# Second values and gates moved into the attention loop's background, later queries placed by transfers, background weights split in one piece

## Chip, cores and metric

The kernel runs on one core of one Trainium2 chip, as one program and one launch. The metric is the device time in microseconds (us), lower is better: the median of several executions. The profile is of one more execution of the same program, with a time of its own.

## What is computed

A decoder trunk of two layers on 512 tokens of width 1024, in float32. Layer A is a gated short convolution and an MLP. Then one shared key/value side is projected (`w_kv`, six parts of 256 columns: raw, selection and window keys and values). Layer B is an attention with 16 heads in 4 groups over three branches, followed by another MLP and a last norm. Cut to what bears on the change:

```python
kv = (h @ w_kv).reshape(B, S, 6, N_KV_GROUPS, HEAD_DIM)
k_cmp = compress_blocks(k_raw, cmp_pe_k, phi_k_w1, phi_k_w2)   # blocks of 32 tokens, stride 16
v_cmp = compress_blocks(v_raw, cmp_pe_v, phi_v_w1, phi_v_w2)   # silu(flat @ w1) @ w2
qg = h @ w_qg                                                  # 1024 query + 48 gate columns
q = qg[..., :1024] * HEAD_DIM ** -0.5
gates = sigmoid(qg[..., 1024:])
# for every query: softmax over compressed blocks, over selected blocks, over the window
o = gt[..., 0:1] * o_c + gt[..., 1:2] * o_s + gt[..., 2:3] * o_w
return o.reshape(B, S, 1024) @ w_o
```

With 512 tokens all selection blocks are taken, so the selection and the window branch are both full causal attentions (`br` 0 and 1) with keys and values of their own.

## The kernel before, in words

Every float32 matmul is made of three float16 matmuls on a high and a low half of each operand. So each weight piece is loaded by a DMA on SP's queue (`load_piece`, L188 to L201, three buffers `wst`), and `convert_piece` (L210) makes its high half on ScalarE (L232, `whi`) and its low half on VectorE (L233, `wlo`, four buffers of each). The list `pieces` (L122 to L140) is the order in which pieces are loaded, converted and used. A piece has 1024 columns per partition, two of them carry 256 output columns of a projection. Pieces with an index below `whole` (L139) are converted in two steps of 512, those from there on in one step of 1024 (`ahead_fine`, L839). Conversion runs two pieces ahead of use.

The attention section starts at L760. A **lead-in** (L1080) runs to its end piece by piece: `keys(0)`, `keys(1)` (selection and window keys into `KD`), `queries(0)` (group 0), `values(0)`, `values(1)` (L865, into `VT`: 96 matmuls of 256 columns, in two accumulation banks, then four evictions of 128x256 on ScalarE and on VectorE, L883 and L884), `gates()` (L887: 96 matmuls of 48 columns, then four sigmoids, L899).

Then the **loop of items** (L1318) starts. An item is one pass of scores for one group, one block of 128 queries, one branch and one, two or four heads (`Full`, L1132, 22 for each group), or one pass over compressed blocks for two groups (`Cmp`, L1207, 8 of them), 96 items in all. Its stages: `st0` makes scores on TensorE into bank `b`, adds the bias on VectorE (L1160) and takes the exponential on ScalarE (L1162); `st1`, two items later, transposes the weights on TensorE into bank `c` (L1168, two banks) and copies the high half on ScalarE (L1171); `st2`, three items later, makes the low half on VectorE (L1174), which frees the bank; `st3`, four items later, multiplies with the values (L1187 to L1189) and, at the end of a block, weights by the gates; `st4`, six items later, turns a finished block for the output projection.

Beside the items runs a **background** (L1303), a chain of generators that is given TensorE work by a credit: in each pass of the loop `credit` rises (L1334) and generators are stepped until it is used up, where a step is worth about its TensorE time in us. The chain: `raw(0)`, `queries(1)`, `phi(0)` alternating with `raw(1)`, `queries(2)`, `phi(1)`, `queries(3)`, and when groups 0 and 1 are finished (mark `o1`) `out_proj(0)`. `raw` (L933) projects raw keys or values, scales them in another order (L946), splits them (L409) and puts them with 12 DMAs (L952 to L954) into the tile `big`, from which `phi` (L960, 96 matmuls of 155 columns) reads. `queries(g)` (L906) makes the query tile `Q` (three buffers): the head's own half by a copy on ScalarE (L917) and the other half by a subtraction (L918) on VectorE for groups 1 and 2, on GpSimd for 0 and 3; these heads stand in a list `later`, and one is taken out in each pass.

The order on each engine is not exactly that of the program: it is set when the program is built, by dependences and readiness. `first_half` and `mlp_down` of the second MLP follow the attention.

## Time and profile before

| | us |
|---|---|
| median of 3 runs | 1106.68 (1106.1 to 1107.04) |
| the profiled execution, its own time | 1106.44 |
| its span | 1104.7 |
| TensorE matmul busy in the span | 1087.0 (98%) |
| VectorE busy | 897.3 (81%) |
| ScalarE busy | 584.0 (53%) |
| GpSimd busy | 57.4 (5%) |
| granted TensorE clock, mean | 0.998 |

How to read it: times are from the span's start. Matmuls are pipelined and their ends are modelled, so a busy TensorE (PE) is not one without gaps: a gap shorter than a matmul's tail does not show as idle. DVE is VectorE, ACT is ScalarE, POOL is GpSimd, SP is the engine whose queue issues most transfers, PEld is the load of a matmul's weights. In a row of `--lines` kind, the numbers after the bar are busy us and mean ns of one instruction, then the engine's idle time before them and what ended it. The lead-in's last part lies between about 521 and 544.8 us, the loop of items between 544.8 and 752 us, the output projection and the second MLP behind that.

### The profile page before, as it was taken

Reading aid. Unit: us, or ns where it says so; the run is one execution under the profiler, and the core shown is the slowest. Engines: PE = TensorE matmul, PEld = TensorE weight load, DVE = VectorE, ACT = ScalarE, POOL = GpSimd, SP = SyncE. Lnnn points to the kernel's source line nnn. Section 1 sums busy time; section 2 is a strip of 40 time slices with the busy share of each in tenths; the row PEclk is TensorE's granted clock in tenths of the full one; section 3 lists DMA queues with packets and bytes.
Section 4 is the critical chain, followed back from the end, with each engine's and each line's share of the span. In section 5 each row is a group of like instructions: output and inputs, shape, how many; then the busy total and the mean of one; then the engine's idle time right before and its main releaser. Section 6 shows DMA issues by size and latency. Waiting matters only on the chain. (4 is left out here: it accounts for less than half of the span.)

```text
span 1104.7 us, 20302 instructions
## 1 busy us (share of the span) xinstructions
PE 1087.0 (98%) x8112; PEld 704.9 (64%) x8112; DVE 897.3 (81%) x1594; ACT 584.0 (53%) x925; POOL 57.4 (5%) x74
## 2 busy tenths in 40 slices
PE   9999999999999999999999999999999999999997
PEld 4446644447884448875767676675444788445886
DVE  5897757987988767979488899996798798875786
ACT  5663245544333544447677887874655534352353
POOL 1000000000000000000100102211100000000022
PEclk9999999999999999999999999999999999999999
DMA  8353135633333333312352432011653333330222
GB/s 254 117 152 115 39 96 153 172 96 115 115 108 106 111 97 108 103 31 76 115 154 68 131 116 79 28 33 57 172 153 115 116 115 115 115 96 1 84 89 77
DMA packets 149710, 115.77 MB, mean 105 GB/s; under 512 B 8828, under 2 KB 146768, under 8 KB 149616
## 3 DMA queue, kind: packets, MB, share of 16 engines
q1 hardware_dynamic: 146720, 109.14, 33.0%
q10 hardware_dynamic: 2512, 4.70, 1.4%
q8 instruction: 64, 1.05, 0.4%
q0 software_dynamic: 384, 0.63, 0.2%
q14 instruction: 30, 0.25, 0.1%
HBM read 110.22 MB, written 2.14 MB: 102 GB/s over the span
## 5 line engine op out<-in xcount | busy, mean ns | idle before, releaser
L232 ACT ACTIVATE whi<-wst 128x1024 f16<-128x1024 f32 (+3 forms) x156 | 136.2, 887 | 120.8 <-PE b L387 37.4
L688 PEld LDWEIGHTS <-whi 128*128 128x128 f16 x1768 | 173.0, 98 | 20.4
L219 ACT ACTIVATE whi<-wst 128x1792 f16<-128x1792 f32 x70 | 118.2, 1696 | 124.6 <-DVE wst L160 55.5
L233 DVE SCALAR_TENSOR_TENSOR wlo<-wst,whi 128x1024 f16<-128x1024 f32 (+3 forms) x156 | 157.1, 1017 | 26.6 <-ACT whi L232 26.3
L388 PEld LDWEIGHTS <-wlo 128*128 128x128 f16 x976 | 95.5, 98 | 105.5 <-issue 0.7
L386 PEld LDWEIGHTS <-whi 128*128 128x128 f16 x976 | 95.7, 98 | 101.0 <-issue 0.9
L387 PEld LDWEIGHTS <-whi 128*128 128x128 f16 x976 | 95.5, 98 | 100.3 <-issue 0.3
L220 DVE SCALAR_TENSOR_TENSOR wlo<-wst,whi 128x1792 f16<-128x1792 f32 x70 | 141.0, 2018 | 15.4 <-ACT whi L219 15.4
L625 DVE TENSOR_TENSOR rl<-ml_z,rh 128x1792 f16<-128x1792 f32 x32 | 64.7, 2023 | 44.5 <-ACT rh L624 44.4
L688 PEld LDWEIGHTS <-wlo 128*128 128x128 f16 x884 | 86.5, 98 | 10.8 <-issue 0.4
L624 ACT ACTIVATE rh<-ml_z 128x1792 f16<-128x1792 f32 x32 | 54.3, 1696 | 60.2 <-DVE ml_z L166 60.2
L1162 ACT ACTIVATE at_p<-at_s,at_m 128x384 f32<-128x384 f32 (+3 forms) x128 | 70.9, 555 | 22.3 <-DVE at_m L1160 21.2
L388 PE MATMUL b<-xsh,wlo 128*128 128x512 f16 x208 | 78.8, 379 | 0.0
L387 PE MATMUL b<-xsl,whi 128*128 128x512 f16 x208 | 78.8, 379 | 0.0
L386 PE MATMUL b<-xsh,whi 128*128 128x512 f16 x208 | 78.8, 379 | 0.0
L386 PE MATMUL c<-xsh,whi 128*128 128x512 f16 x192 | 72.8, 379 | 0.0
L387 PE MATMUL c<-xsl,whi 128*128 128x512 f16 x192 | 72.8, 379 | 0.0
L388 PE MATMUL c<-xsh,wlo 128*128 128x512 f16 x192 | 72.8, 379 | 0.0
L158 DVE TENSOR_TENSOR wst<-wst 128x512 f32<-128x512 f32 x70 | 48.5, 695 | 26.5 <-DMA wst<-mlp_w_dram 25.2
L688 PE MATMUL a<-rh,whi 128*128 128x256 f16 x256 | 69.1, 273 | 0.0
L688 PE MATMUL a<-rh,wlo 128*128 128x256 f16 x256 | 69.1, 273 | 0.0
L688 PE MATMUL c<-rh,whi 128*128 128x256 f16 x252 | 68.7, 273 | 0.1
(388 smaller groups left out, 2686.8 us busy)
## 6 DMA issues: line engine op xcount, KB each, us to landing
wst<-mlp_w_dram SPq DMA_DIRECT2D x256, 256.0 KB, 3.4
wst<-a_w_in_dram SPq DMA_DIRECT2D x12, 512.0 KB, 3.8
wst<-w_kv_dram SPq DMA_DIRECT2D x12, 512.0 KB, 3.8
wst<-a_w_out_dram SPq DMA_DIRECT2D x8, 512.0 KB, 3.4
wst<-b_w_qg_dram SPq DMA_DIRECT2D x8, 512.0 KB, 3.7
wst<-b_w_o_dram SPq DMA_DIRECT2D x8, 512.0 KB, 3.4
T<-ext_d ACTq DMA_DIRECT2D x6, 528.0 KB, 3.9
wst<-a_w_in_dram SPq DMA_DIRECT2D x12, 256.0 KB, 3.0
```

Source lines behind the costliest of these rows:

```text
L158: DVE.tensor_tensor(b[:, :, 4:7:2], b[:, :, 0:1].to_broadcast(two), b[:, :, 2:0:-1], op=OP.add)
L219: ACT.activation(hi, b[:, :, 1:], AF.Copy, scale=sc)
L220: lows[0] = DVE.scalar_tensor_tensor(lo, b[:, :, 1:], sc, hi, op0=OP.mult, op1=OP.subtract)
L232: ACT.activation(hi[:, s:e], w, AF.Copy, scale=sc)
L233: DVE.scalar_tensor_tensor(lo[:, s:e], w, sc, hi[:, s:e], op0=OP.mult, op1=OP.subtract)
L386: PE.matmul(ps, w[0], xs[0], start=start, stop=False, **k)
L387: PE.matmul(ps, w[0], xs[1], start=False, stop=False, **k)
L388: return PE.matmul(ps, w[1], xs[0], start=False, stop=stop, **k)
L624: ACT.activation(rh[0][:, p], z[:, 1:8], AF.Copy)
L625: DVE.tensor_tensor(rh[1][:, p], z[:, 1:8], rh[0][:, p], op=OP.subtract)
L688: mm = PE.matmul(acc7[i], wl if n == 1 else wh, xl if n == 2 else xh, stop=c == closes[i] and n == 2, start=c == 0 and n == 0 and not othe ...
L1162: self.weighed = ACT.activation(self.p[:, w], lg[:, w], AF.Exp, bias=mn[:, j:j + 1], scale=-1.0, accum_out=l[:, br * 4 + h:br * 4 + h + 1])
```

## The change

Two projections leave the lead-in and become the background's first: `values(1)` and `gates()`. A new check `need_last` lets a window item wait for them, in program order, before its `st3`. The background's order becomes `values(1)`, `gates()`, `queries(1)`, `raw(0)`, `phi(0)` alternating with `queries(2)`, `raw(1)`, `phi(1)`, `queries(3)`, `out_proj(0)`; the piece list is put into the same order. The credit per pass becomes 1.25 (items 0 to 53), 1.0 (to 63) and 0.75 instead of 1.14 (0 to 43), 0.9 (to 49) and 0.58. The first four `Cmp` items move from behind places 4, 7, 10, 13 of group 2 to behind 9, 11, 14, 16 (items 54, 57, 61, 64). For groups 1 to 3 a query tile's halves are made for two heads at a time on all 128 partitions (two copies, two subtractions) into `kr_hl`, and four DMAs on SP's queue put them in place. `raw` loses a memset and one of three DMAs of each group. `whole` moves from `queries(3)`'s pieces to those of `values(1)`, so all the background's pieces are converted in one step.

```diff
@@ -122,21 +122,21 @@
     block(b_w_qg[0], 0)
-    for part in (3, 5):
-        block(w_kv, part * 256)
+    block(w_kv, 3 * 256)
+    whole = len(pieces)
+    block(w_kv, 5 * 256)
     cols(b_w_qg[0], 1024, 48, SW)
+    block(b_w_qg[0], 256)
     block(w_kv, 0)
-    block(b_w_qg[0], 256)
     for k in (0, 8):
         block(phi_k_w1, 0, SW, k, 4)
-        cols(w_kv, 256, 256, SW, k // 2, 4)
+        cols(b_w_qg[0], 512, 256, SW, k // 2, 4)
         block(phi_k_w1, 0, SW, k + 4, 4)
     cols(phi_k_w2, 0, 64, SW, 0, 2)
-    block(b_w_qg[0], 512)
+    block(w_kv, 256)
     block(phi_v_w1, 0, SW, 0, 16)
     cols(phi_v_w2, 0, 64, SW, 0, 2)
-    whole = len(pieces)
     block(b_w_qg[0], 768)
@@ -886,15 +886,18 @@
         def gates():
             w = next_piece()
+            cv = ahead_fine()
             pg = abank()
             for t in range(4):
                 for c in range(8):
+                    next(cv, None)
...
-                yield
+                yield 0.6
+            drain(cv)
@@ -915,16 +918,30 @@
-                (POOL if g in (0, 3) else DVE).tensor_tensor(q[o, h], t[r, m], q[r, h], op=OP.subtract)
+                POOL.tensor_tensor(q[o, h], t[r, m], q[r, h], op=OP.subtract)
                 done.add(f"q{g}.{h}")
+            def two_heads(m, hl):
+                ACT.activation(hl[:, 2 * m], t[:, m], AF.Copy)
+                (POOL if g == 3 else DVE).tensor_tensor(hl[:, 2 * m + 1], t[:, m], hl[:, 2 * m], op=OP.subtract)
+            def put_heads(hl):
+                for s in range(2):
+                    r, o = slice(64 * s, 64 * s + 64), slice(64 - 64 * s, 128 - 64 * s)
+                    nc.sync.dma_start(q[r, s::2], hl[r, 0::2])
+                    nc.sync.dma_start(q[o, s::2], hl[r, 1::2])
+                done.update(f"q{g}.{h}" for h in range(4))
...
-            for h in range(4):
-                if lead_in[0]:
+            if lead_in[0]:
+                for h in range(4):
                     head(h)
-                else:
-                    later.append(lambda h=h: head(h))
+            else:
+                hl = ap.tile([128, 4, S], F16, name="kr_hl", bufs=1)
+                for m in range(2):
+                    later.append(lambda m=m: two_heads(m, hl))
+                later.append(lambda: put_heads(hl))
@@ -934,7 +951,6 @@
-            DVE.memset(kr[64:128, :, 0:4, S - 1:S], 0.0)
@@ -951,7 +967,6 @@
                     nc.sync.dma_start(kr[64:128, :, g, 0:S - 32], hl[r, :, 32:S])
-                    nc.sync.dma_start(kr[64:128, :, g, S - 32:S - 1], hl[r, :, 1:32])
@@ -1024,7 +1039,7 @@
-        done = set()
+        done = {"v0"}
@@ -1077,7 +1092,7 @@
-        for k in (keys(0), keys(1), queries(0), values(0), values(1), gates()):
+        for k in (keys(0), keys(1), queries(0), values(0)):
             drain(k)
@@ -1139,6 +1154,9 @@
+            def need_last(self):
+                return [f"v{self.br}"] + (["gates"] if self.br else [])
@@ -1295,16 +1316,18 @@
-        items += mixed(full(2), {4 + 3 * qb: Cmp(0, qb) for qb in range(4)})
+        items += mixed(full(2), {i: Cmp(0, qb) for qb, i in enumerate((9, 11, 14, 16))})
...
         def background():
+            yield from marked("v1", values(1))
+            yield from marked("gates", gates())
+            yield from queries(1)
             yield from raw(0)
-            yield from queries(1)
-            yield from in_turn(phi(0), raw(1))
-            yield from queries(2)
+            yield from in_turn(phi(0), queries(2))
+            yield from raw(1)
             yield from marked("cmp", phi(1))
...
-            credit += 1.14 if i < 44 else 0.9 if i < 50 else 0.58
+            credit += 1.25 if i < 54 else 1.0 if i < 64 else 0.75
...
+                        if s == 3:
+                            have(items[j].need_last())
                         getattr(items[j], f"st{s}")()
```

## Rows read from the trace of the kernel before

**Rows 1.** The page: busy us of each engine over the span.
```profile
PE 1087.0 (98%) x8112; PEld 704.9 (64%) x8112; DVE 897.3 (81%) x1594; ACT 584.0 (53%) x925; POOL 57.4 (5%) x74
```

**Rows 2.** Windows, items 0-21, 22-43, 44-63, 64-69, 70-95: length, busy us by engine.
```profile
544.80:596.20 51.40, 50.67 (x496) 33.71 (x492) 41.23 (x112) 40.38 (x104) 1.86 (x3) 1.00 0.40 114
596.20:648.00 51.80, 49.75 (x574) 36.41 (x573) 47.50 (x137) 42.29 (x121) 4.18 (x5) 1.00 0.40 116
648.00:688.00 40.00, 38.16 (x484) 28.19 (x482) 39.31 (x119) 32.28 (x88) 6.61 (x10) 1.00 0.34 106
688.00:699.20 11.20, 9.08 (x113) 6.80 (x113) 9.88 (x31) 10.40 (x27) 6.93 (x7) 1.00 0.03 11
699.20:752.00 52.80, 51.97 (x615) 37.97 (x615) 50.93 (x159) 40.05 (x114) 9.11 (x14) 1.00 0.10 32
```

**Rows 3.** Groups of PE by shape, 544.8 to 752 us: first, typical and large ones.
```profile
L1168 PE MATMUL c<-ident,at_p 128*128 128x128 f32 x316 | 49.7, 276 | 5.6 <-DVE at_pl L1174 3.5 <-DVE big L409 0.9 <-ACT whi L232 0.7
L1187 PE MATMUL d<-VT,at_ph 128*128 128x64 f16 x311 | 37.9, 193 | 1.0 <-ACT at_ph L1171 0.7 <-DVE o_t L1105 0.2
...
L386 PE MATMUL a<-xqh,whi 128*128 128x512 f16 x48 | 18.2, 379 | 0.0
...
L386 PE MATMUL e<-big,whi 128*128 128x155 f16 x64 | 13.9, 233 | 0.0
```

**Rows 4.** Timeline of PE around 600 us: start, length, line; matmuls following without a gap.
```profile
599.97 0.60 PE L1168 MATMUL c<-ident,at_p 128*128 128x128 f32 x4
600.41 0.19 PE L1187 MATMUL d<-VT,at_ph 128*128 128x64 f16 x1
...
600.76 0.33 PE L1152 MATMUL b<-KD,Q 128*128 128x384 f16 x1
...
601.50 0.38 PE L386 MATMUL a<-xsh,whi 128*128 128x512 f16 x1
601.72 0.38 PE L387 MATMUL a<-xsl,whi 128*128 128x512 f16 x1
```

**Rows 5.** Groups of PE by shape, 531.5 to 545 us: second values and gates.
```profile
L874 PE MATMUL b<-whi,xsh 128*128 128x256 f16 x32 | 8.7, 272 | 0.0
...
L894 PE MATMUL c<-whi,xqh 128*128 128x48 f16 x32 | 2.5, 183 | 0.0
```

**Rows 6.** Groups of DVE by shape, 544 to 752 us: conversions and query heads.
```profile
L233 DVE SCALAR_TENSOR_TENSOR wlo<-wst,whi 128x512 f16<-128x512 f32 x26 | 17.3, 687 | 2.7 <-ACT whi L232 2.7
...
L233 DVE SCALAR_TENSOR_TENSOR wlo<-wst,whi 128x1024 f16<-128x1024 f32 x9 | 10.9, 1209 | 0.2 <-ACT whi L232 0.2
...
L918 DVE TENSOR_TENSOR Q<-q_t,Q 64x512 f16<-64x512 f32 x8 | 5.5, 686 | 0.2
```

**Rows 7.** Timelines of SP and DMA groups: the puts of raw(0), raw(1); us to landing.
```profile
561.89 0.66 SPq L952 DMA_DIRECT2D big<-kr_hl  x1
...
569.75 0.62 SPq L954 DMA_DIRECT2D big<-kr_hl  x1
...
big<-kr_hl SPq DMA_DIRECT2D x8, 128.0 KB, 2.3
```

**Rows 8.** Timeline of PE: raw(0)'s last matmuls and phi(0)'s first.
```profile
558.16 0.38 PE L388 MATMUL a<-xsh,wlo 128*128 128x512 f16 x1
...
580.49 0.23 PE L386 MATMUL e<-big,whi 128*128 128x155 f16 x1
```

**Rows 9.** Timeline of ACT at the end of the lead-in: the two table loads.
```profile
544.49 1.28 ACT L899 ACT_TABLE_LOAD   x1
545.78 1.24 ACT L899 ACTIVATE GT<-c,zero,rtok 128x48 f32<-128x48 f32 x4
547.04 1.28 ACT L1162 ACT_TABLE_LOAD   x1
```

**Rows 10.** Timelines of ACT and PE at 691 to 694 us: queries(3)'s heads and a stall.
```profile
691.77 1.92 ACT L917 ACTIVATE Q<-q_t 64x512 f16<-64x512 f32 x3
...
694.23 0.20 PE L1187 MATMUL d<-VT,at_ph 128*128 128x64 f16 x1 [0.49 <-ACT at_ph L1171]
```

More of the change, by code (lines that the diff above doesn't have):

```diff
@@ L1214, in need, with need_last @@
                 return [f"q{2 * self.gp}.3", f"q{2 * self.gp + 1}.3", "cmp"]
+            def need_last(self):
+                return []
             def st0(self):
@@ L1315, in body, with have @@
         bg = background()
+        def have(names):
+            for k in names:
+                while k not in done:
+                    if later:
+                        later.pop(0)()
+                    elif next(bg, "end") in ("wait", "end"):
+                        raise RuntimeError(k)
         lead = {1: 2, 2: 3, 3: 4, 4: 6}
@@ L1320, in body @@
             if i < len(items):
-                for k in items[i].need():
-                    while k not in done:
-                        if later:
-                            later.pop(0)()
-                        elif next(bg, "end") in ("wait", "end"):
-                            raise RuntimeError(k)
+                have(items[i].need())
                 items[i].st0()
```

## Prediction

> **What bounds the kernel now.** I read the page first: matmuls are busy for 98% of the span [rows 1], so the same matmuls in another order can only gain where TensorE waits. Next the windows of the item loop [rows 2], because every edit is there or flows into it. The reader is to see two columns. PE is idle for 7.6 us of 207.2 (0.7, 2.1, 1.8, 2.1 and 0.8 in the five windows). DVE is at 80, 92, 98, 88 and 96% of them. So from item 22 on VectorE is nearly full, and TensorE waits for it.
>
> The idle column is too small, since a matmul's shown length covers gaps. So I counted [rows 3, 4]. The steps from one start to the next are 0.11 us for a transpose (0.44 / 4), 0.029 for 64 columns (0.35 / 12) and 0.216 for 512; the other shapes go by columns, not under 0.025. The groups of the loop's 207.2 us hold 360 transposes (316 for the weights, 28 and 16 others), 956 of 64 columns (three lines like the one of 311, and 24), 383 of 512 (three lines each of 48, 32 and about 27, and 64 score matmuls), 192 of 155, and 384-, 256-, 128-column and small ones for 29.9 us. Sum: 39.6 + 27.7 + 82.7 + 12.6 + 29.9 = 192.5 us. **TensorE loses 14.7 us in the loop**, twice its idle column. That is all that this change can win; outside, the lead-in's stretch from 500 to 545 us is busy throughout. By the idle column the loss is spread as about 1.4, 4.0, 3.5, 4.1 and 1.6 us. The longest named wait is a transpose waiting for the low half of an earlier item's weights, which VectorE makes and which frees bank `c` (3.5 of the 5.6 us in the first row of [rows 3]). In the fourth window there is no background: `queries(3)` is done and the mark `o1` not yet there, and 4.1 of 11.2 us are lost.
>
> **The change, part by part.**
>
> *Second values and gates.* 96 matmuls of 256 columns and 96 of 48 leave the lead-in [rows 5]: 96 x 0.109 + 96 x 0.025 = 10.5 + 2.4 = 12.9 us. They come back whole in the loop, 192.5 + 12.9 = 205.4 us. The sum of that alone is nothing: both places are TensorE's. The gain is indirect, as the same VectorE work is spread over more TensorE time.
>
> *VectorE's work in the loop*, 188.8 us now (sum of the DVE column of [rows 2]). Heads of groups 1 and 2: eight subtractions of 0.69 become four on twice the partitions, at the same length as they have the same columns: -2.7. Evictions of the second values: about +1.5 (four of 256 columns, at most half of a 1024-column step's 1.209 [rows 6], in part still before the loop). Conversion: a piece in two steps costs 2 x 0.687 = 1.37, in one 1.209 [rows 6]: -0.16 for each of 16 pieces, -2.6 by lengths and -1.3 by start-to-start steps, as neighbours overlap by 0.08. Two or three pieces that were converted in the lead-in move into the loop: +2.4 to +3.6. Sum about 0 to +2: some 190 us on 205 us of matmuls, 0.93, against 188.8 on 192.5, 0.98.
>
> *Where it falls.* By credits, items 0 to 21 get 3 + 22 x 1.25 = 30.5 us of background (28.1 before), 22 to 43 27.5 (25.1), 44 to 63 22.5 (13.5), the end 0.75 per item instead of 0.58. `values`, `gates` and `queries` need little of VectorE, so items 0 to 21 stay easy. In 22 to 43 VectorE falls to roughly 0.88 of TensorE's work and in 44 to 63 to roughly 0.97 (its own items and the moved `Cmp` items, with `raw(1)` and `phi(1)` in front). Between the windows' 80% with 2.7% lost and 92% with 7.7%, I take 5% and 7%: 2.6 of 4.0 and 3.1 of 3.5 (on 51.7 and 44.4 us). The first window gives 0.3, the last nothing measurable. Relief: 1.4 + 0.4 + 0.3 = **2.1 us**. From below it could be 0 (the stalls are bursts, whatever the mean), from above all that exceeds the first window's 2.7%: 14.7 - 5.5 = 9.2.
>
> *Heads and puts.* The copies of three heads in a row hold ScalarE for 1.92 us and TensorE then waits for the next weights' high half [rows 10]; two full copies in two passes replace them. I take **-0.7 us** (that stall is 0.49, and a second such one is likely among 12 head copies that become 6). The four puts cost SP 4 x 0.61 and land 2.3 us later [rows 7], about 5 us, behind at most one weight load. By the credits the puts are issued in passes 19, 41 and 67, three items ahead of items 22, 44 and 70; an item takes 1.9 to 2.4 us, so the first two are covered. The third also waits for GpSimd, and item 70 may come 0 to 1.5 us late; I take 0.3. If that cover were gone, each put would cost up to its 5 us. The dropped transfers free SP of 8 x 0.61; a queue that is not the bound.
>
> *`phi` right behind `raw`.* This adds a wait. Before, `raw(0)`'s last matmul starts at 558.2, its first put is issued at 561.9, the last at 569.75, landing 2.3 later, and `phi(0)` begins only at 580.5 [rows 7, 8]: ten us of `queries(1)` hide it. Now `phi(0)` and `phi(1)` follow at once. With 8 puts instead of 12 the last lands at about 561.9 + 8 x 0.65 + 2.3 = 569.4, **11 us after the matmul**. `phi(0)` has `queries(2)` beside it: the half that its first weight piece allows, 5.2 us, and the items' own 5 us, cover it. `phi(1)` has nothing beside it: `queries(3)`'s pieces stand behind `phi_v`'s four and there are four `whi`. In those 11 us the items run alone, as in the fourth window, where 4.1 of 11.2 us are lost. But the filler is not gone: `queries(3)` then runs later, into items 64 to 71, which by the credits have none (eight items against five before). Between 0 and +4.1, I take **+1.5**.
>
> *Gates among exponentials.* The sigmoid now comes between exponentials: one table load more on ScalarE, 1.28 us [rows 9], beside 1.24 of sigmoids; and the bank of the gates is wanted by `queries(1)`'s second accumulation right behind. ScalarE is at 79% in that window [rows 2]. Between 0 and +3.7 (the loads and sigmoids wholly in TensorE's way), I take **+0.9**. In the row the sigmoid starts 0.01 us after its load ends. The Trainium skill (ScalarE: Activation LUTs, section What ACT_TABLE_LOAD costs) adds a drain of about 1.38 us to each load; the row has none, and by the page this term would be up to 1.4 larger.
>
> Sum: -2.1 - 0.7 + 0.3 + 1.5 + 0.9 = -0.1 us from the middle values. The two ends are not alike: the relief can grow to 9.2, while the two new waits partly move filler to where it lacks (the fourth window's 4.1 us falls with them). For that I take off another 1.3 us, a third of those 4.1: **-1.4 us**. The profiled execution took 1106.44, of which 1104.7 is the span; it is 0.24 under the median of 1106.68. So 1105.0 for it, **1105.3** on the median's level.
>
> **Rivals.** (1) *The filler evens it out.* If TensorE loses everywhere near 4% of its 205 us, between the first window's 2.7% and the second's 7.7%, 8.5 us remain of 14.7: -6.2, 1100.5. For it: the loss follows VectorE's share in the windows. Against: the fourth window's cause, no background, stays. (2) *`phi(1)` starves, slower.* The 11 us pass without filler at the fourth window's price, 4.1, and `phi(0)`'s cover fails by 1, while relief is only the bursts' 0.7: +4.4, 1111.1. It decides as soon as the gap from `raw(1)`'s last to `phi(1)`'s first matmul exceeds what the items can run ahead, about 6 us. (3) *The sigmoids are taken apart.* Evictions of values run in the trace as each quarter is ready; if the four sigmoids do so too, each exponential between them costs two loads, 2.6 us. Three such pairs are 7.7 us on an engine with 11 us of room in 51 [rows 2], all at one spot: about +3, 1109.7. (4) *Whole pieces burst.* A conversion of 1.21 instead of 0.69 us stands before the low half that frees a bank; 16 pieces at 0.1 to 0.2 us take the relief away: +0.5, 1107.2. The Trainium skill (Perfetto Trace Analysis, Optimizing Scalar/DVE Operations) says that grouping pays on a saturated engine and that breaking instructions up may help where an engine causes bubbles without being full: here the last three windows are of the first kind and the first of the second. (5) *Nothing arrives:* the stalls are bursts, 0.
>
> **How the numbers follow.** Chances: forecast 0.45 (own range -4 to +1.5), rival 1 0.22, rival 2 0.18, rival 3 0.07, rivals 4 and 5 0.08. About 0.2%, 2.2 us, is what a measurement of this kernel tells from no change. Of the forecast 0.17 lies below -2.2, the rest within; rival 1 gives nearly all to faster, rivals 2 and 3 most to slower. Faster 0.39, same 0.39, slower 0.22. Range 1100.0 to 1110.2: rival 1 inside but for its far half, rival 2 up to a little under its middle; no more than 2 in 10 stay out.
>
> **What would show it.** Right: DVE under 92% of items 22 to 43; PE idle in the loop under 7 us although the loop holds 205 us of matmuls. The gap between `raw(1)` and `phi(1)` about 11 us with some 2 us of idle PE in it. Three loads of tables around the gates, not five or more. Items 22, 44 and 70 starting without a wait for a DMA. Wrong: PE idle over 3 us behind `raw(1)`; idle before item 70; or `queries(3)` so late that the fourth window moves to the loop's end.

## Result: 1106.6 us before, 1113.5 us after

| | before | after |
|---|---|---|
| median, us | 1106.62 (1106.1 to 1107.04) | 1113.53 (1112.49 to 1113.95) |
| ratio to before | | 1.0062 [1.0049, 1.0075] |
| the profiled execution, its span, us | 1106.44, 1104.7 | 1113.35, 1111.6 |
| matmul work counted by steps, us | 1074.3 | 1074.3 |
| TensorE's loss (starts less steps), us | 21.4 | 28.0 |

The change makes the kernel 6.9 us slower. The matmuls are the same, so all of it is loss, counted as in the prediction: the time from one matmul's start to the next, less the step of its shape. Over the whole execution the loss rises by 6.6 us. A count over all matmuls, cut at the first score matmul of an item, places it:

| loss, us | lead-in and all ahead | items 0-21 | 22-43 | 44-69 | 70-95 | behind the loop |
|---|---|---|---|---|---|---|
| before | 5.5 | 1.0 | 3.5 | 7.1 | 3.0 | 1.2 |
| after | 5.8 | 2.4 | 2.0 | 10.7 | 3.4 | 3.7 |

The gain hoped for is there, 1.5 us in items 22 to 43. Three places take more than it gives: items 0 to 21, where the gates now are, the stretch around the second compression (44 to 69), and a place outside the loop that the prediction did not look at.

The windows of after for the same five groups of items as [rows 2] (length, then busy us of PE, PEld, DVE, ACT and POOL, the granted clock with 1.00 as 2.4 GHz, DMA share, GB/s):

```profile
532.20:587.10 54.90, 53.27 (x603) 38.92 (x602) 40.60 (x112) 45.95 (x107) 2.71 (x3) 1.00 0.34 99
587.10:640.60 53.50, 52.47 (x581) 37.69 (x580) 45.65 (x125) 40.79 (x110) 4.16 (x5) 1.00 0.41 120
640.60:692.60 52.00, 47.42 (x555) 35.17 (x554) 45.10 (x120) 35.22 (x94) 7.70 (x10) 0.97 0.42 123
692.60:702.55 9.95, 8.94 (x113) 6.87 (x110) 9.52 (x31) 8.48 (x23) 3.74 (x3) 1.00 0.24 55
702.55:758.45 55.90, 54.80 (x623) 39.02 (x622) 53.43 (x164) 41.63 (x115) 10.42 (x15) 1.00 0.13 39
```

VectorE's share of the second window falls from 92% to 85%, and PE's idle part with it, 2.1 to 1.0 us. In the third PE is idle for 4.6 us instead of 1.8, and the clock is under 1.00, which no window of before shows. The waits of TensorE's matmuls in and behind the loop, longest sums first (us in total, times, longest):

```profile
PE b L1170 <- DVE at_m L1178: 2.6, 3, 1.7
PE b L386 <- DVE X L591: 2.3, 1, 2.3
PE c L1186 <- DVE at_pl L1192: 2.1, 3, 1.2
PE d L1205 <- ACT at_ph L1189: 1.1, 2, 0.6
PE a L386 <- ACT GT L902: 1.0, 1, 1.0
```

The second line is one wait, behind the loop; the fifth is the gates'. The first and third hold the two long waits between 649 and 655 us (1.7 and 1.2 us).

**Behind the loop.** The timeline of PE at the start of the second MLP:

```profile
783.19 0.38 PE L387 MATMUL c<-xsl,whi 128*128 128x512 f16 x1
785.83 0.38 PE L386 MATMUL b<-xsh,whi 128*128 128x512 f16 x1 [2.26 <-DVE X L591]
```

The MLP's first pair accumulates in bank `b`, and that bank still holds the output projection's last sums, which VectorE is adding to `X`. In the kernel before the last projection pair uses `c` and `a`, and the MLP's first matmul starts at 778.31 without a wait:

```profile
778.10 0.38 PE L388 MATMUL a<-big,wlo 128*128 128x512 f16 x1
778.31 0.38 PE L386 MATMUL b<-xsh,whi 128*128 128x512 f16 x1
```

The lead-in's calls for banks go round in "aabbcc" (`acc`, two banks of each letter in turn); the second values took two and the gates one. In the loop they take bank `a` without counting, so the round stands three calls off when the output projection comes, while the MLP starts its own count anew.

**The gates.** ScalarE's timeline (idle time before and its cause in brackets), and PE's at the wait:

```profile
551.58 1.28 ACT L902 ACT_TABLE_LOAD   x1
552.88 0.39 ACT L902 ACTIVATE GT<-a,zero,rtok 128x48 f32<-128x48 f32 x1
553.66 1.28 ACT L1180 ACT_TABLE_LOAD   x1
556.62 1.28 ACT L902 ACT_TABLE_LOAD   x1
557.92 0.95 ACT L902 ACTIVATE GT<-a,zero,rtok 128x48 f32<-128x48 f32 x3
559.27 1.28 ACT L1180 ACT_TABLE_LOAD   x1
```

```profile
558.92 0.38 PE L386 MATMUL a<-xqh,whi 128*128 128x512 f16 x1 [0.96 <-ACT GT L902]
```

One sigmoid stands apart from the other three, with four exponentials between them: four table loads where before had two [rows 9]. `queries(1)`'s second accumulation waits for the gates' bank.

**Behind `raw(1)`.** Its last matmul starts at 646.80, `phi(1)`'s first at 662.13. What lies between, on VectorE and SP (the first and the last of eight puts):

```profile
647.02 1.98 DVE L962 TENSOR_TENSOR q_t<-a,rb 128x512 f32<-128x512 f32 x2
649.40 1.21 DVE L233 SCALAR_TENSOR_TENSOR wlo<-wst,whi 128x1024 f16<-128x1024 f32 x1
651.60 1.81 DVE L409 TENSOR_TENSOR kr_hl<-q_t,kr_hl 128x512 f16<-128x512 f32 x2
```

```profile
652.33 0.60 SPq L968 DMA_DIRECT2D big<-kr_hl  x1
656.93 0.61 SPq L969 DMA_DIRECT2D big<-kr_hl  x1
```

So 15.3 us, not the forecast 11. The first put is issued 5.5 us behind the last matmul, not 3.7 as for `raw(0)` in [rows 7, 8]: between scaling and splitting VectorE has 2.6 us of other work (a bias, the whole weight piece, a low half and a weighting of the items), where it had 1.0 us there. The last put lands 2.3 us behind its issue, at 659.2, which is 12.4 us behind the last matmul. The other 2.9 us are not the puts': `phi(1)`'s first matmul shows no wait for them, and until 662.1 TensorE is at matmuls of the items, which stand ahead of it in its order. In the gap the items run alone and wait for VectorE, and PE is idle for 3.9 us. Then the clock goes (windows, columns as above):

```profile
650.00:652.50 2.50, 0.99 (x15) 0.76 (x15) 2.50 (x5) 1.74 (x5) 0.75 (x1) 1.00 0.20 34
652.50:655.00 2.50, 0.99 (x9) 0.62 (x9) 2.50 (x7) 0.71 (x2) 0.36 (x1) 0.98 0.96 283
655.00:657.50 2.50, 2.50 (x29) 2.18 (x27) 1.84 (x7) 1.71 (x5) 0.00 (x0) 0.50 0.85 198
657.50:660.00 2.50, 2.50 (x45) 2.42 (x44) 1.62 (x10) 1.88 (x8) 0.00 (x0) 0.84 0.45 104
660.00:662.50 2.50, 1.96 (x35) 1.53 (x32) 1.94 (x12) 2.50 (x13) 0.26 (x1) 1.00 0.00 0
```

VectorE is full for five us while PE has 0.99 us of work in each 2.5. Behind that the granted clock stands at 0.50, the lower level, for 3.4 us. The windows then show a full PE, but its matmuls take about twice their steps: 1.7 us more are lost.

### The profile page after: what moved, and what is told of

Same layout as the page of the kernel before. It is cut to its first block, busy times and chain, and to the rows that moved or that the text cites. A ratio compares the mean times of both kernels' runs of the same rounds, so it can differ in the third digit from the quotient of the medians.

```text
span 1111.6 us, 20296 instructions
## 1 busy us (share of the span) xinstructions
PE 1090.0 (98%) x8112; PEld 707.5 (64%) x8112; DVE 895.6 (81%) x1571; ACT 584.6 (53%) x905; POOL 57.1 (5%) x72
## 4 chain that ended last, share of the span: by engine, by line
PE 89%; DVE 4%; ACT 4%; issue 2%; DMA 0%; ACTq 0%; DVEq 0%
PE a L688 8%; PE c L688 7%; PE b L688 6%; PE a L386 6%; PE a L388 6%; PE a L387 6%; PE b L386 5%; PE b L387 5%; PE b L388 5%; PE c L388 5%; PE c L386 5%; PE c L387 5%; PE d L688 4%; PE c L1186 2%; PE e L688 2%
## 5 line engine op out<-in xcount | busy, mean ns | idle before, releaser
L232 ACT ACTIVATE whi<-wst 128x1024 f16<-128x1024 f32 (+5 forms) x139 | 134.5, 974 | 138.4 <-PE b L387 51.6
L233 DVE SCALAR_TENSOR_TENSOR wlo<-wst,whi 128x1024 f16<-128x1024 f32 (+5 forms) x139 | 155.6, 1124 | 25.5 <-ACT whi L232 25.3
L688 PE MATMUL c<-rl,whi 128*128 128x256 f16 x252 | 68.7, 273 | 0.0
```

The lines of the kernel that those rows point to most:

```text
L232: ACT.activation(hi[:, s:e], w, AF.Copy, scale=sc)
L233: DVE.scalar_tensor_tensor(lo[:, s:e], w, sc, hi[:, s:e], op0=OP.mult, op1=OP.subtract)
L688: mm = PE.matmul(acc7[i], wl if n == 1 else wh, xl if n == 2 else xh, stop=c == closes[i] and n == 2, start=c == 0 and n == 0 and not othe ...
```

## Experiments

Three theories stand against each other for each place: the cause just read; that the loss is VectorE's bound and comes back wherever one mends it; and that another part of the change costs. All times are medians; the kernel before is 1106.3 to 1106.6 in each series. Losses, waits and windows are of the one profiled execution of a kernel, which can lie off its median: 1110.84 in `e2_before_rotation`, 1118.11 in `e10_order`, 1118.06 in `e3_products_ahead`, 1110.12 in `e19_third_puts`, 1109.22 in `e22_filler_between`.

### The hand-over to the MLP

`e1_rotation` is the changed kernel, `e2_before_rotation` the kernel before, with one line more:

```diff
         lead_in[0] = False
+        turn[0] += 3
```

> The changed kernel with one line more: behind the lead-in the counter that deals out the accumulation banks goes on by three, the number of banks that the second values and the gates used to take there. Theory of the hand-over (the last pair of the output projection and the first pair of the MLP both get bank b, because the count is out of step): the 2.4 us stall at 783 us is gone and nothing else moves, 2.2 to 2.6 us less than the changed kernel, about 1111.1. Rival (the stall there is the square sums of X that the MLP needs anyway, whatever the bank): within 0.5 us of the changed kernel, about 1113.5, with the stall at another line.

> The kernel before with the same one line, so that its count is out of step as the changed kernel's is. Theory of the hand-over: it alone costs 2.2 to 2.6 us, about 1109.0, with a wait of some 2.3 us of PE at the MLP's first product. Rival (the stall belongs to what the change did elsewhere): no difference, 1106.6 within 0.5.

Measured 1110.57 (-3.0 from 1113.53) and 1108.92 (+2.3, ratio 1.0026 [1.0015, 1.0037]). The kernel before then has the wait too:

```profile
PE b L386 <- DVE X L591: 2.3, 1, 2.3
```

In `e1_rotation` the loss behind the loop is 1.3 us, as in the kernel before, and each group of items loses what it lost, within 0.2. Shown in both directions: the count alone costs 2.3 to 3.0 us. The wait itself is 2.3 us. In the profiled execution of `e2_before_rotation` the granted clock is also at half for 3.4 us right behind it, and the loss behind the loop is 4.1 us more than in the kernel before:

```profile
782.30:785.70 3.40, 3.40 (x10) 1.22 (x9) 3.40 (x6) 2.22 (x4) 0.41 (x1) 0.50 0.99 276
```

Three of this kernel's seven times lie at 1110.3 to 1110.8, the other four at 1108.4 to 1108.9. In the trace of after the same wait leaves the clock at 1.00.

### The gates

`e4_gates_lead` puts the gates back into the lead-in and leaves the count as it is in the changed kernel; `e13_gates_rot` mends both.

```diff
-        for k in (keys(0), keys(1), queries(0), values(0)):
+        for k in (keys(0), keys(1), queries(0), values(0), gates()):
...
-            yield from marked("gates", gates())
```

> The changed kernel with the gates alone put back into the lead-in (the count of banks set so that it stands as in the changed kernel from there on). Theory of the sigmoids taken apart (four loads of tables among the exponentials, a wait of 0.96 and one of 0.62 us for them on TensorE): two loads, items 11 to 22 lose about 0.1 instead of 1.5 us, 1 to 1.6 us saved, about 1112.2. Rival (these items lose because the second values' and gates' banks are wanted by the second queries, whoever fills them): under 0.5 us saved. Rival (2.4 us of easy TensorE work leave the loop, and VectorE's stretches pay for it): the saving is given back between items 22 and 64, total within 0.5 us.

> The changed kernel with two causes mended: gates in the lead-in, and the count of banks put back into step. If the two add up (hand-over 3.0 as measured by itself, gates 1 to 1.6), 4.0 to 4.6 us under the changed kernel, about 1109.3; if the gates' saving is given back elsewhere, about 1110.5.

Measured 1111.13 (-2.4) and 1108.34 (-5.2, ratio 1.0017 [1.0007, 1.0026]). The causes add up: 3.0 and 2.4 singly, 5.2 together. Items 0 to 21 lose 0.7 instead of 2.4 us; there is one table load each way again. The 2.4 us are 0.8 more than was expected at most, and items 22 to 69 change as well: behind `raw(1)` the clock now holds. That it holds because the background, without the 2.4 us of gates' matmuls, runs ahead by some items is argued, not shown. The same place in `e13_gates_rot`:

```profile
642.40:647.50 5.10, 4.17 (x48) 3.00 (x47) 5.07 (x11) 3.77 (x10) 0.72 (x1) 1.00 0.00 0
647.50:650.00 2.50, 1.09 (x18) 0.76 (x17) 2.50 (x6) 0.77 (x4) 0.00 (x0) 1.00 0.76 233
650.00:652.50 2.50, 2.30 (x37) 1.62 (x34) 2.38 (x8) 2.42 (x7) 0.47 (x1) 1.00 0.88 224
```

One stretch of 2.5 us with 1.09 us of matmuls, not two in a row, and no fall; it is no rule, since in `e3_products_ahead` below one such stretch is followed by a fall. The gap is 12.2 us (643.8 to 656.0), and `phi(1)` starts 0.4 us behind the last landing. Items 44 to 69 lose 9.2 instead of 10.7, of which the clock's 1.7 are more than all; items 22 to 43 lose 0.7 more.

### The second compression and its filler

Four kernels on the changed one. `e10_order` puts the order of the background back (in `background` and in `pieces`). `e3_products_ahead` draws the last queries' 48 products ahead of `phi(1)`; `e11_three_mended` is `e13_gates_rot` with the same. `e16_half_ahead` is `e13_gates_rot` with 24 of them (eight steps of `last_q` instead of all). The weight pieces of what is drawn ahead move with it in `pieces`. The first diff below is `e10_order`'s, the second that of the other three. A fifth kernel, `e3_filler`, with all of `queries(3)` ahead, has no time.

```diff
-            yield from queries(1)
             yield from raw(0)
-            yield from in_turn(phi(0), queries(2))
-            yield from raw(1)
+            yield from queries(1)
+            yield from in_turn(phi(0), raw(1))
+            yield from queries(2)
             yield from marked("cmp", phi(1))
```

```diff
             yield from raw(1)
+            last_q = queries(3)
+            for u in last_q:
+                if u == "wait":
+                    break
+                yield u
             yield from marked("cmp", phi(1))
-            yield from queries(3)
+            yield from last_q
```

> The changed kernel with the order of the background put back: first keys' raw products, then the second queries, then the first compression in turn with the second raw products, then the third queries, then the second compression; second values and gates stay in the background ahead of them. Theory of the starved compression (the second one stands right behind its own raw products and waits for their copies, so that ten items go without background and the clock halves for 3.4 us): items 44 to 54 lose 2 us instead of 6, the clock stays at full, and 3 to 4.5 us are saved: 1109 to 1110.5. Rival (those items are bounded by VectorE, which has the same work in either order): under 1 us saved, 1112.5 or more. Rival (the order put back starves the first compression instead): no saving, with a new stall near 590 us.

> The changed kernel with one thing moved: the 48 products of the last queries (10.4 us of TensorE) come between the second raw products and the second compression, and their sums stay in their two banks until the first compressed scores are done, as they wait now. Theory of the starved compression (no background for ten items behind the second raw products, since the compression waits for their copies; clock at half for 3.4 us): the stretch of items 44 to 54 loses 2 to 3 us instead of 5.9, the clock stays at full, and 2.5 to 4 us are saved against the changed kernel, 1109.5 to 1111. Rival (the stretch is bounded by VectorE, 16.6 us busy of its 19.2): it loses as much, and less than 1 us is saved. Rival (the filler is only moved: what items 44 to 54 win, items 64 to 70, now without it, lose): items 54 to 70 lose 2 us more, total within 1 us.

> The changed kernel with all three causes mended: gates in the lead-in, the count of banks in step, and the last queries' products ahead of the second compression. If the three are the whole of the loss, 6.5 to 8.5 us under the changed kernel, 1105 to 1107, level with the kernel before or a little under it, since the relief of items 22 to 44 (1.5 us) stays. Rival (a cause that none of the three touches, such as the transfers of the queries or the conversion in whole pieces, costs as well): 1108 or more.

> The changed kernel with gates in the lead-in and the count of banks in step (as the kernel at 1108.34), and besides it half of the last queries' products (24 of 48, 5.2 us) ahead of the second compression, the other half behind it as now. Theory of the scarce filler (between the second raw products and the mark o1 there are only the compression and the last queries to put beside items that VectorE bounds; all queries ahead emptied items 54 to 70, none ahead empties items 44 to 54, and the loss grows with the length of a stretch without filler): items 44 to 54 lose 2 to 3 instead of 4.2, items 54 to 70 lose 5 to 6.5 instead of 5.0, total 0.5 to 2 us under that kernel, 1106.3 to 1107.8. Rival (any product put into the gap delays the compression, and this alone costs): slower in proportion, half of the 6.8 us that all of them cost there, about 1111.7.

| | us | loss in items 0-21 | 22-43 | 44-69 | clock at half |
|---|---|---|---|---|---|
| after | 1113.53 | 2.4 | 2.0 | 10.7 | once |
| `e10_order` | 1117.09 | 3.8 | 4.7 | 10.0 | twice, and once behind the loop |
| `e3_products_ahead` | 1119.41 | 2.4 | 2.0 | 16.0 | twice |
| `e13_gates_rot` | 1108.34 | 0.7 | 2.7 | 9.2 | no |
| `e11_three_mended` | 1115.18 | 0.7 | 2.7 | 15.6 | twice |
| `e16_half_ahead` | 1107.61 | 0.7 | 2.7 | 8.5 | no |

My theory was half right, and its cure made the kernel 6 to 7 us slower where 2.5 to 4 us were to be saved. With the products in the gap, items 44 to 53 lose 1.4 instead of 5.9 us, as it said. But then nothing is left for the items behind: 54 to 69 lose 14.7 instead of 4.8. Windows of `e3_products_ahead` (items 44 to 53 first):

```profile
639.80:672.05 32.25, 31.41 (x330) 22.20 (x329) 23.50 (x64) 20.38 (x56) 2.10 (x3) 1.00 0.35 100
672.05:677.50 5.45, 3.81 (x67) 2.96 (x65) 5.10 (x12) 4.54 (x15) 0.00 (x0) 1.00 0.75 226
677.50:680.00 2.50, 1.08 (x19) 0.79 (x18) 2.50 (x9) 1.28 (x5) 0.87 (x2) 1.00 0.41 137
680.00:683.20 3.20, 3.20 (x39) 2.98 (x38) 2.90 (x8) 2.08 (x4) 0.00 (x0) 0.51 0.02 5
683.20:692.85 9.65, 7.33 (x90) 5.32 (x89) 8.89 (x25) 6.31 (x15) 2.09 (x3) 0.99 0.31 111
692.85:707.10 14.25, 11.13 (x126) 8.92 (x125) 12.89 (x37) 9.39 (x26) 5.20 (x5) 0.88 0.17 40
```

The first line has VectorE at 73% and PE at 97%; from 672 us on VectorE is at 90 to 100% and PE starves, with the clock at half around 681 and again around 702. The third line is the counterexample from above: 1.08 us of matmuls in 2.5, behind 3.81 in 5.45, and then the fall. Filler between `raw(1)` and the mark `o1` is a fixed amount, `phi(1)` and `queries(3)`; as I read it, what counts is that no long stretch is without any. Half of the products ahead is the best of the three, 0.7 us under none (items 44 to 53 lose 1.2 instead of 4.2, the others 7.3 instead of 5.0). That the order of before cures it was wrong as well: with the second values in front, `queries(1)` and `queries(2)` are not done when items 22 and 44 want them and are pulled in by force (6.3 us of background in item 43 alone).

Two kernels on `e13_gates_rot` change only the puts: `e19_third_puts` has the third put of each group and the memset back, `e17_two_queues` issues the second of the two on GpSimd's queue.

```diff
-                    nc.sync.dma_start(kr[64:128, :, g, 0:S - 32], hl[r, :, 32:S])
+                    nc.gpsimd.dma_start(kr[64:128, :, g, 0:S - 32], hl[r, :, 32:S])
```

> The kernel at 1108.34 with one part of the change undone: the third put of each group of raw products and its memset are back, four issues of 0.61 us more. By the theory of the wait for the puts the gap grows from 12.2 to some 14.7 us and the time by 0.5 to 1.5 us, to about 1109.3. Rival (the gap is set by VectorE and by the order that was fixed at build time): within 0.4 of 1108.3.

> The kernel at 1108.34 with the two puts of each group of raw products on two queues, the first on SP's, the second on GpSimd's. By the theory of the wait for the puts the last lands some 2.4 us earlier (four issues of 0.61 us fewer in a row), so the gap from the second raw products to the second compression, 12.2 us, becomes about 9.8, and 0.5 to 1.5 us are saved: about 1107.3. Rival (the gap is set by VectorE, which scales and splits the sums late, and by the items between): gap and time as they are, 1108.3 within 0.4. Rival (GpSimd starts its transfers later than SP): a longer gap, slower.

`e19_third_puts`: 1110.55, +2.2, more than the 0.5 to 1.5 expected; the gap grows from 12.2 to 14.3 us, items 44 to 69 lose 1.0 more in the profiled execution. `phi(1)` again starts right behind the last landing (658.0 and 658.1). So the puts do set the gap in these two kernels, and it costs. `e17_two_queues`: 1113.32, +5.0, slower as only its last rival said, and with a shorter gap, as that one didn't say: 11.5 us, but each put takes longer: 3.9 and 3.6 us from issue to landing at `phi(0)` (2.4 and 2.3 in `e13_gates_rot`) and 4.5 and 4.6 at `phi(1)` (3.4 and 3.2). TensorE, whose order is fixed when the program is built, stands before `phi(0)`:

```profile
PE e L386 <- DMA big<-kr_hl: 1.9, 1, 1.9
```

and behind `raw(1)` the clock falls to half from 651 to 654 us. That the puts of the two queues hinder each other is argued from these times, not shown: other transfers run beside them, and with SP alone single puts of `raw`, of 120 or 128 KB, took from 2.3 to 5.2 us (kernel before, `e21_transfers_whole`).

### The parts that need no new order, in the kernel before

`e6_before_puts`: queries of groups 1 to 3 two heads at a time, put by four transfers. `e20_before_transfers`: also no third put and memset in `raw`. `e21_transfers_whole`: also `whole` moved to the values' pieces. `e5_before_whole`: the kernel before with `whole` alone. The edits are the lines of the diff shown ahead.

> The kernel before with one part of the change alone: queries of groups 1 to 3 made for two heads at a time on all partitions and put in place by four transfers. The prediction's own term: 0.7 us less for the three copies in a row on ScalarE and 2.7 us less of VectorE's work, 0.3 more for the third group: 1105.9 to 1106.3. Rival (puts arrive late for items 22, 44 and 70, or the one buffer kr_hl that raw products and queries now share makes them wait for each other): 0.5 to 2 us slower, about 1107.8.

> The kernel before with the queries of groups 1 to 3 put by transfers (1104.73 by itself) and also without the third put of each group of raw products and its memset. Theory (in that order of the background each compression has ten us of queries in front, so the wait for the puts is covered): nothing, 1104.7 within 0.4. Rival (shorter series of puts also let weight loads through on SP's queue earlier): 0.5 us less.

> The kernel before with one part of the change alone: all of the background's weight pieces are converted in one step of 1024 instead of two of 512. The prediction: 1.3 us less of VectorE's work, worth 0 to 0.5 us, 1106.2 to 1106.7. Rival (whole pieces burst: a conversion of 1.21 us stands before the low half that frees a bank): 0.5 to 1 us slower, about 1107.3.

> The last kernel with the background's pieces converted in one step besides. If the parts add up: 1104.7 plus what whole pieces cost or give in the kernel before by themselves. Rival (with less of VectorE's work the bursts no longer matter, or matter more): a different sign here.

| | us | ratio to before | loss in items 0-21 | 22-43 | 44-69 |
|---|---|---|---|---|---|
| before | 1106.5 | | 1.0 | 3.5 | 7.1 |
| `e6_before_puts` | 1104.73 | 0.9983 [0.9974, 0.9992] | 1.0 | 1.8 | 6.1 |
| `e20_before_transfers` | 1103.91 | 0.9977 [0.9968, 0.9986] | 1.0 | 1.6 | 6.1 |
| `e5_before_whole` | 1107.05 | 1.0005 [0.9996, 1.0014] | 1.1 | 3.3 | 7.5 |
| `e21_transfers_whole` | 1104.0 | 0.9975 [0.9965, 0.9985] | 1.0 | 1.8 | 6.1 |

The transfers of the queries alone give 1.8 us, more than the 0.4 of the term, and, with the dropped puts, 2.6, where the theory of `e20_before_transfers` had nothing and its rival 0.5. By the count 1.7 us come in items 22 to 43, where the change had its gain, and 1.0 in 44 to 69; where the dropped puts' 0.8 come, the traces do not show. Whole pieces give nothing that can be told. The window of items 22 to 43 in `e6_before_puts`, and the wait for the low half that frees bank `c` there, before and in `e6_before_puts`:

```profile
596.40:646.65 50.25, 49.36 (x575) 36.63 (x574) 45.71 (x136) 40.58 (x118) 4.17 (x5) 1.00 0.44 123
```

```profile
PE c L1168 <- DVE at_pl L1174: 2.0, 4, 0.6
PE c L1182 <- DVE at_pl L1188: 0.8, 2, 0.5
```

Against [rows 2] VectorE has 1.8 us less to do and ScalarE 1.7; no run tells which of the two it is. But the relief seen in after is there without any second values in the loop: it is the transfers', not that of more TensorE time beside the same VectorE work.

### What is left: second values in the loop

From `e21_transfers_whole` (1104.0) to `e13_gates_rot` (1108.3) are 4.3 us: second values in the background, and the order, places and credit that came with them. `e24_values_alone` moves only the values, with a credit of 1.38 up to item 43; `e26_values_early` has 1.48 instead. `e22_filler_between` is `e13_gates_rot` with another order and credit. `e25_thin_filler` is `e20_before_transfers` with a credit of 0.52 for 0.58 in items 50 to 69. The diffs are of `e24_values_alone` and of `e22_filler_between`.

```diff
         def background():
+            yield from marked("v1", values(1))
             yield from raw(0)
...
-            credit += 1.14 if i < 44 else 0.9 if i < 50 else 0.58
+            credit += 1.38 if i < 44 else 0.9 if i < 50 else 0.58
```

```diff
             yield from queries(1)
             yield from raw(0)
-            yield from in_turn(phi(0), queries(2))
-            yield from raw(1)
+            yield from in_turn(phi(0), raw(1))
+            yield from queries(2)
```

> The changed kernel with gates in the lead-in and the count of banks in step (1108.34), and an order of the background in which queries stand between each raw products and its compression again, while the second queries stay early: second values, second queries, first raw products, first compression in turn with the second raw products, third queries, second compression, last queries; the credit is 1.35 a pass up to item 43, 0.8 to 53, 0.65 to 69, so that the third queries are done when item 44 wants them. Theory of the starved compression (the loss that is left comes from its place right behind its raw products, and no product needs to be pulled forward by force here): no ten items without background, items 44 to 70 lose 7 us as in the kernel before instead of 9.2, total 1105.0 to 1106.5. Rival (what is left comes from the denser background in the items up to 43, or from the moved compressed scores): 1108 or more.

> The kernel at 1104.0 (the kernel before with the transfers and whole pieces) and the second values moved into the background's front, nothing else: gates stay in the lead-in, the order of the rest, the compressed scores and the credit from item 44 on stay, the credit up to item 43 is 1.38 so that the same work is done by then, the count of banks is in step. Theory of the relief (the same VectorE work spread over more TensorE time): items 0 to 43, which lose 2.8 us there, lose 1 to 2 us, so 1 us less, 1103. Rival (the transfers have already taken what there was to win, and the denser background only brings bursts): 0.5 to 3 us slower, about 1106; then the order that the change gives the rest and its place of the compressed scores cost the other 2 to 3 us up to 1108.3.

> The last kernel but one (second values alone in the background, 1108.89) with the credit 1.48 instead of 1.38 a pass up to item 43, so that the third queries are done some three items earlier; there item 44 waits 3.9 us for their transfers and items 43 and 44 lose 5.9 us. Theory (second values in the background cost by themselves nothing, they only make the third queries late): the waits for the transfers are gone and the time is 1104 to 1105, that of the kernel without the move, 1104.0. Rival (the denser background costs what the later items then lack): 1106 or more, with the loss in items 44 to 70 instead.

> The kernel at 1103.91 (the kernel before with the transfers) with the credit 0.52 instead of 0.58 a pass in items 50 to 69, so that the last queries reach some two items further. Theory of the scarce filler (a stretch that VectorE bounds loses less if the filler is spread over all of it): items 64 to 70 lose 2.0 to 2.5 instead of 2.7, total 0.3 to 0.7 us less. Rival (the third group's transfers then come late for item 70): 0.5 us slower or more.

| | us | background in items 0-43, us | 44-69 | loss 0-21 | 22-43 | 44-69 |
|---|---|---|---|---|---|---|
| `e21_transfers_whole` | 1104.0 | 52.2 | 14.0 | 1.0 | 1.8 | 6.1 |
| `e22_filler_between` | 1110.57 | 63.1 | 13.5 | 0.8 | 6.6 | 5.5 |
| `e24_values_alone` | 1108.89 | 63.5 | 13.1 | 1.6 | 5.4 | 6.2 |
| `e26_values_early` | 1109.68 | 66.9 | 9.8 | 2.4 | 2.4 | 10.0 |
| `e13_gates_rot` | 1108.34 | 57.7 | 19.0 | 0.7 | 2.7 | 9.2 |
| `e25_thin_filler` | 1103.55 | 52.2 | 14.6 | 1.0 | 1.6 | 6.1 |

`e22_filler_between` has no starved compression: items 44 to 69 lose 5.5 us, less than the 7 of its theory, but the time is its rival's. What that saves, the items ahead lose: the third queries come late for item 44 (a wait of 2.2 us for their puts). `e24_values_alone` has the same, larger, and the granted clock falls to half in that wait:

```profile
PE b L1168 <- DMA Q<-kr_hl: 3.9, 1, 3.9
```

```profile
652.10:655.50 3.40, 2.78 (x20) 2.42 (x21) 0.56 (x2) 1.08 (x2) 0.00 (x0) 0.50 0.24 79
```

With more credit (`e26_values_early`) this wait is down to 0.6, and my theory of that run, that the move by itself costs nothing, falls: 1109.68. Items 0 to 43 lose 4.8 us, more than the 2.8 without the values, and 44 to 69 lose 10.0. What is spent early lacks late. Its two windows, items 22 to 43 and 44 to 69, and below them those of `e21_transfers_whole`:

```profile
594.20:652.40 58.20, 56.47 (x649) 42.30 (x650) 48.15 (x130) 43.21 (x115) 2.67 (x5) 1.00 0.53 148
652.40:702.25 49.85, 43.40 (x546) 31.84 (x545) 47.19 (x141) 38.99 (x107) 12.04 (x14) 1.00 0.22 66
```

```profile
596.15:646.40 50.25, 49.34 (x575) 36.69 (x574) 45.16 (x129) 40.19 (x112) 4.17 (x5) 1.00 0.43 123
646.40:696.55 50.15, 46.95 (x596) 34.97 (x594) 48.90 (x145) 41.70 (x111) 11.21 (x14) 1.00 0.33 102
```

The second window takes 50 us in both, with 43.4 us of PE in the one and 47.0 in the other: less TensorE work there is no shorter time, and VectorE, busy for 47 to 49 of the 50 us, is the likely bound. The first window has PE nearly full in both, so 7 us more of work there are 8 us more of time, although VectorE's share falls from 90% to 83%. All eight kernels with the second values in the loop and banks and gates mended end at 1107.6 (`e16_half_ahead`) to 1115.2 (`e11_three_mended`); none reaches 1104. Whether some other order would is open. The fastest kernel is `e25_thin_filler`, 1103.55, ratio 0.9973 [0.9963, 0.9983], without any of the moves; the interval holds the ratio of `e20_before_transfers`, 0.9977. Its theory is not borne out: items 64 to 69 lose 2.7 us as without it.

## Why the prediction was wrong

The forecast was 1105.3, the result lies 8.2 us above it and outside the range. Three steps of it failed. The largest is the relief with the new order: the second values in the loop, booked at -1.9 us in all, cost 4.3. The hand-over of banks was in no term and costs 2.3 to 3.0. The gates, booked at +0.9, cost 2.2 to 2.4. The ladder of kernels, each one step from the one above, gives the terms:

| step | us | change | my term |
|---|---|---|---|
| before | 1106.5 | | |
| queries put by transfers (`e6_before_puts`) | 1104.7 | -1.8 | -0.7 + 0.3 |
| no third puts (`e20_before_transfers`) | 1103.9 | -0.8 | 0 |
| whole pieces (`e21_transfers_whole`) | 1104.0 | +0.1 | in the relief |
| second values, order, places, credit (`e13_gates_rot`) | 1108.3 | +4.3 | -2.1 + 1.5 - 1.3 |
| gates in the loop (`e1_rotation`) | 1110.6 | +2.2 | +0.9 |
| count of banks out of step (after) | 1113.5 | +3.0 | none |

- *"Outside, the lead-in's stretch from 500 to 545 us is busy throughout"*, so the loop was all that I looked at. That holds for what can be won, not for what can be lost. Work was taken out of the lead-in and its matmuls costed, but not the state it leaves, here the count that deals out banks to everything behind. 2.3 to 3.0 us, in no term and no rival.
- *Relief, -2.1.* Items 22 to 43 did lose 1.5 us less, as forecast (1.4), and VectorE's share fell to 85% (0.88 forecast). The cause was another: the transfers alone do it in the kernel before, so that the numbers agree is luck. I booked one gain under two terms. What failed is the step from VectorE's share to TensorE's loss: in `e26_values_early` the share of that window is 83% against 90% in `e21_transfers_whole`, and it loses 2.4 us against 1.8. Nor did VectorE's work stay the same: it rose by 5.5 us in the loop (188.8 to 194.3) where I had 0 to +2, and my own terms add up to -1.4 to +1.1. Conversions gave +3.3, evictions +2.4, heads -2.7, the rest +2.5. In items 44 to 63 the gain of 0.4 became a loss of 4.4, nearly all of it (4.1) in the gap of the next point. Of the -1.3 for the fourth window 0.8 came (items 64 to 69, next point).
- *`phi` right behind `raw`, +1.5 of 0 to 4.1.* Rival 2 was the mechanism, and its price was at the upper bound: items 44 to 53 lose 4.1 us more. 1.7 of it is the clock, which no row of before shows. The gap was 15.3 instead of 11 us. I took the delay to the first put from `raw(0)`, 3.7 us; `raw(1)` itself has 5.1 us in the trace of before (614.9 to 620.0), and 5.5 came. The landing of 2.3 us in [rows 7] is a median, and `raw(0)`'s last put took 4.7. `phi(0)`'s cover held, as forecast. That it would be paid back in items 64 to 69, which lose 2.6 instead of 3.4, was right in sign.
- *Gates, +0.9 of 0 to 3.7.* Rival 3's form, with one pair of loads more instead of three: +2.2 to 2.4. I had the row that shows evictions taken apart and gave the rival 0.07.
- *Heads and puts, -0.4.* Right in sign, a fourth to a fifth of the -1.8 that came; the dropped puts, costed at nothing, gave another 0.8. No item waited for its puts in after, as forecast; in `e24_values_alone`, where the cover is gone, two did, for 1.0 and 3.9 us (I had said up to 5).
- *Whole pieces.* Neither the 1.3 us of VectorE nor rival 4's bursts can be told from nothing.
- *The signs that I named.* VectorE under 92% in items 22 to 43: right. PE idle in the loop under 7 us: 9.4. Gap 11 us: 15.3. Three table loads: four. PE idle over 3 us behind `raw(1)`, a sign of being wrong: 3.9.

The result lies 8.2 us above the forecast: 3.0 for the banks, 1.3 for the gates, 6.2 for the second values and their order, less 2.1 that the transfers and whole pieces gave beyond their terms. That is 8.4 by the ladder, whose steps come from different series. What in the 6.2 us is the gap behind `raw(1)` and what the denser loop is not settled: each order that mended the one paid with the other.

## What to carry to other kernels

Work that is moved out of a place leaves counts behind (banks, buffers, queues): follow what takes the next one, up to the end of the kernel, before the move is costed at nothing. Filler for a stretch that another engine bounds was worth something only there and spread over all of it; brought into a stretch that had TensorE full already, it bought no time in any order tried here. A step put right behind the one that feeds it makes a hole as long as the copy between them. A lower mean share of the bounding engine is not yet a smaller loss. And try the parts alone: here the parts without a new order beat both kernels.

## What the runs showed of the hardware

- In after, behind two stretches of 2.5 us with 0.99 us of matmuls each, the granted clock stood at 1.2 GHz for 3.4 us, and the matmuls in it took about twice their steps: 1.7 us lost beyond the stall itself. In `e13_gates_rot`, where one stretch of 1.09 us in 2.5 stood between fuller ones, the clock held; in `e3_products_ahead` it fell behind one of 1.08 us in 2.5 that followed 3.81 us in 5.45. Behind the wait of 2.2 to 2.3 us at the hand-over it fell in the traces of `e2_before_rotation` and `e10_order` and held in those of after, `e3_products_ahead` and `e4_gates_lead`. What decides between the two is open. The Trainium skill (TensorE: Matmul & The Clock Gate, section HAM oscillation — how this bites in real kernels) tells of waits between bursts of matmuls that make the next burst start at the lower clock, at a price of half the time spent there. The trace of after agrees, 1.7 of 3.4 us, though there no single wait was longer than 1.73 us and matmuls ran between them.
- With the puts of `raw(1)` issued on two queues at a time each took longer to land (medians 4.5 and 4.6 us, against 3.4 and 3.2 with all on one), and four issues fewer in a row brought the dependent matmul forward by 0.7 us, where 2.4 was expected. Whether the second queue or the other transfers of that time are the cause is not shown.
